# Two transformer layers on one core: the opening written out block by block, nine and ten leading tiles, and large shared tiles

## The chip, the cores and the metric

The kernel runs on one core of a Trainium2 chip. Its time is the device time of one execution in microseconds (us); of several runs the median is given. The core has engines with instruction queues of their own: TensorE (PE in the profile, with PEld for its weight loads), VectorE (DVE), ScalarE (ACT), GpSimd (POOL), and the queue that issues the transfers (SP). Semaphores tie them together. Each engine takes its instructions in order, so an instruction that waits holds up all that stand behind it in its queue.

## The reference

Sixteen meta tokens are put ahead of 512 tokens, which gives L = 528 rows of width 1024. Each of two layers does this to the rows h:

```python
proj = rmsnorm(h, pre_mix_norm) @ w_in           # 1024 x 3600
#  columns: rq rk rv rg (retention, 4 heads of 128), gq gk gv gr (gated linear attention, 4 heads), ga (16 wide)
merged = concat(retention(rope(rq), rope(rk), rv) normed * silu(rg),
                gla(gq, gk, gv, decay from ga) normed * silu(gr))
h = h + rmsnorm(merged @ w_out, post_mix_norm)
u = rmsnorm(h, pre_ffn_norm) @ ffn_up            # 1024 x 5632
a, g = split(conv3(u))                           # causal, width 3, per column
h = h + rmsnorm((gelu(a) * g) @ ffn_down, post_ffn_norm)
```

RMSNorm divides each row by the root of its mean square and multiplies it by a gain for each column. The output is h without the meta tokens.

## The kernel before, in words

Activations lie transposed: 128 columns of the model on the partitions (KD = 8 blocks k of them), tokens along the row. Every wide product is made of three half-precision products, since weights and activations are each split into a high and a low half (`product`, L361 to L363: high*high, high*low, low*high; each over the eight blocks k, so 24 matmuls for a tile of 128 output columns). The tokens go in two parts, 0 to 232 and 232 to 528 (`SPLIT`), because a product of all 528 doesn't fit one bank of the accumulator. A weight block of 1024 x 128 is loaded as 512 KB into a stage buffer (`Block.load`, L89) and made a "unit" by ScalarE (high half, L105) and VectorE (low half, L106). The ten-odd units ahead of the current one are fetched early (`AHEAD`).

At the start of each layer's mixer the first `LEAD` = 7 tiles of the projection are multiplied with the first part of the tokens alone, and only then with the second part; after them each tile takes both parts in turn (`seq` in `mixer`). The tile list begins with the narrow tile ga (`project_rank`, L540: 16 matmuls), then gk, gk, gq, gq, and four gv; the tenth is the first rk, whose eviction applies the rotation tables. While the second part's norm is still being worked out, the leading tiles are TensorE's work. In layer 0 the norm of the input is special: `start` loads the rows, squares them (`squares`), forms 1/rms on GpSimd (`rstd`, L300), scales the rows by it (`ys`, L408 and L409), transposes the scaled rows block by block (`first_part`, L437), and evicts them as high and low halves of xh with the gain. Tokens 256 to 528 go another way (`first_xh`): the raw rows are transposed into h (`raw_h`, L483), the norms are spread over the partitions by a product of ones with a diagonal (`spread`, L462 and L463), and h is multiplied by them (`scaled`, L471, then `split`, L304 and L305). The raw first part is transposed into h as well, later. At the end of each layer `norms` does the same for the residual: sums of squares over columns (`sumsq`, L327 to L332), `token_rstd` (L316, L300, L462, L463), addition to h on GpSimd (L347), and again for the next norm.

Order: a scheduler with a model of the times sets the order of each engine's queue, from the order in which the program writes the work and from its own clock. In `start` alone the written order is kept, for ScalarE, VectorE and SP, not for TensorE. The load of the identity matrix (`constants`, L242) stands ahead of that region, so the scheduler places it.

Memory: a pool `gen` has 41 slots of one size, out of which nearly everything is taken (rows of the input, projections, `m`, `u`, `ca` and `cg` of the convolution, `ffa`, the tables); `keep` holds xh; `small` has short rings for each name.

## Time and profile before

| | |
|---|---|
| median of 3 runs | 1273.3 us (1272.73 to 1276.95) |
| the profiled execution, its own time | 1271.71 us |
| its span | 1269.8 us |
| TensorE busy | 1239.7 us (98%) |
| VectorE, ScalarE, GpSimd busy | 819.8, 642.0, 167.6 us |
| mean granted TensorE clock | 0.992 |

A chain of waits is the work that ended last, followed back from the end. A group of instructions is all that come from one line with one shape; "mean" is the time of one. Matmuls overlap, so a matmul row of 0.26 us may stand every 0.10 us: the step from one start to the next is what a matmul costs. TensorE's clock is granted at full (1.0) or half rate (0.5).

### The profile page before, as it was taken

The page shows a single profiled execution, that of the slowest core. Times are in us where ns is not written, and L with a number is a line of the kernel's source. Part 1 is how long each engine was busy: PE and PEld are TensorE (multiplying, and loading weights), DVE is VectorE, ACT ScalarE, POOL GpSimd, SP SyncE. Part 2 cuts the span into 40 slices and gives each one's busy share as a digit, 9 for nine tenths or more (in the row PEclk, how much of TensorE's full clock was granted, in tenths as well). Part 3 has the DMA queues.
Part 4 walks back from the last instruction along what each step waited for, and adds up shares of the span by engine and source line. Part 5 has one row for each costly group of instructions (what it writes and reads, how often), then busy time and mean ns, then how long its engine had stood idle before and what let it go on. Part 6 is the DMA issues. An engine that isn't in the chain of part 4 may idle for free.

```text
span 1269.8 us, 26401 instructions
## 1 busy us (share of the span) xinstructions
PE 1239.7 (98%) x11090; PEld 1019.8 (80%) x11090; DVE 819.8 (65%) x1510; ACT 642.0 (51%) x1200; POOL 167.6 (13%) x218
## 2 busy tenths in 40 slices
PE   8999999999999999999988999999999999999997
PEld 6777788888788888888876787888898888886443
DVE  5578845457876666512286688454478867887875
ACT  6664444354855555423255644343548656664541
POOL 1013310044000000000141132100430000000000
PEclk8999999999999999999998999999999999999999
DMA  9731222222433342214152322222215333304651
GB/s 258 212 87 55 68 67 67 68 72 63 133 102 98 101 125 79 88 47 120 32 139 67 84 68 68 64 68 71 84 50 146 108 102 103 126 1 165 200 191 67
DMA packets 206971, 124.26 MB, mean 98 GB/s; under 512 B 6704, under 2 KB 194276, under 8 KB 206852
## 3 DMA queue, kind: packets, MB, share of 16 engines
q1 hardware_dynamic: 206692, 122.04, 32.6%
q8 instruction: 87, 1.43, 0.5%
q0 software_dynamic: 160, 0.52, 0.2%
q14 instruction: 32, 0.26, 0.1%
HBM read 120.45 MB, written 2.10 MB: 97 GB/s over the span
## 4 chain that ended last, share of the span: by engine, by line
PE 80%; DVE 8%; ACT 3%; issue 3%; POOL 2%; DMA 1%; SPq 1%; DVEq 0%; POOLq 0%; ACTq 0%
PE pu L362 12%; PE pu L363 12%; PE pu L361 12%; PE pj L361 6%; PE pj L363 6%; PE pj L362 6%; PE pl L1047 5%; PE pd L362 3%; PE pd L361 3%; PE pd L363 3%; PE po L361 2%; PE po L362 2%; PE po L363 2%; DVE unit L106 2%; PE o L590 1%
## 5 line engine op out<-in xcount | busy, mean ns | idle before, releaser
L362 PE MATMUL pu<-xh,unit 128*128 128x296 f16 (+2 forms) x1408 | 385.7, 275 | 2.0 <-DVE xh L305 2.0
L363 PE MATMUL pu<-xh,unit 128*128 128x296 f16 (+2 forms) x1408 | 385.7, 275 | 0.0
L361 PE MATMUL pu<-xh,unit 128*128 128x296 f16 (+2 forms) x1408 | 384.0, 275 | 0.8 <-ACT xh L304 0.8
L106 DVE SCALAR_TENSOR_TENSOR unit<-st,unit 128x1024 f16<-128x1024 f32 (+1 forms) x186 | 227.5, 1226 | 214.5 <-ACT unit L105 207.8
L361 PEld LDWEIGHTS <-unit 128*128 128x128 f16 x2912 | 285.8, 98 | 48.8 <-issue 5.6
L363 PEld LDWEIGHTS <-unit 128*128 128x128 f16 x2912 | 285.6, 98 | 45.5 <-issue 2.9
L362 PEld LDWEIGHTS <-unit 128*128 128x128 f16 x2912 | 286.3, 98 | 44.5 <-issue 2.2
L105 ACT ACTIVATE unit<-st 128x1024 f16<-128x1024 f32 (+1 forms) x186 | 191.7, 1034 | 138.7 <-PE pu L363 48.7
L361 PE MATMUL pj<-xh,unit 128*128 128x296 f16 (+2 forms) x896 | 248.6, 279 | 1.8 <-ACT gaT L541 1.8
L363 PE MATMUL pj<-xh,unit 128*128 128x296 f16 (+2 forms) x896 | 248.8, 278 | 0.0
L362 PE MATMUL pj<-xh,unit 128*128 128x296 f16 (+2 forms) x896 | 248.6, 278 | 0.0
L934 ACT ACTIVATE u<-pu 128x296 f32<-128x296 f32 (+2 forms) x176 | 66.2, 379 | 99.3 <-PE pu L363 99.2
L363 PE MATMUL pd<-ffa,unit 128*128 128x232 f16 (+1 forms) x352 | 96.8, 276 | 0.0
L361 PE MATMUL pd<-ffa,unit 128*128 128x232 f16 (+1 forms) x352 | 96.8, 276 | 0.0
L362 PE MATMUL pd<-ffa,unit 128*128 128x296 f16 (+1 forms) x352 | 96.7, 276 | 0.0
L332 POOL TENSOR_TENSOR acc<-acc,sq 128x296 f32<-128x296 f32 (+2 forms) x36 | 32.4, 900 | 344.8 <-ACT sq L330 344.1
L300 POOL TENSOR_TENSOR rs_r<-rs_t,every 128x1 f32<-128x1 f32 (+5 forms) x33 | 37.2, 1131 | 279.5 <-DVE rs_t L297 99.5
L923 DVE SCALAR_TENSOR_TENSOR ca<-u,every,ca 128x527 f32<-128x527 f32 (+1 forms) x88 | 66.8, 759 | 10.8 <-ACT ca L918 9.6
L363 PE MATMUL po<-merged,unit 128*128 128x296 f16 (+2 forms) x256 | 69.9, 275 | 0.0
L362 PE MATMUL po<-merged,unit 128*128 128x296 f16 (+2 forms) x256 | 69.9, 275 | 0.0
L923 DVE SCALAR_TENSOR_TENSOR cg<-u,every,cg 128x527 f32<-128x527 f32 (+1 forms) x88 | 66.6, 757 | 4.9 <-ACT cg L918 4.3
L361 PE MATMUL po<-merged,unit 128*128 128x296 f16 (+2 forms) x256 | 69.6, 275 | 0.0
(218 smaller groups left out, 1535.6 us busy)
## 6 DMA issues: line engine op xcount, KB each, us to landing
st<-in_ffn_up SPq DMA_DIRECT2D x88, 512.0 KB, 3.8
st<-in_w_in SPq DMA_DIRECT2D x56, 512.0 KB, 4.0
st<-in_ffn_down SPq DMA_DIRECT2D x46, 512.0 KB, 3.9
st<-in_w_out SPq DMA_DIRECT2D x16, 512.0 KB, 3.6
st<-in_ffn_down SPq DMA_DIRECT2D x8, 384.0 KB, 5.5
out<-yo SPq DMA_DIRECT2D x8, 256.0 KB, 2.0
xt<-in_x SPq DMA_DIRECT2D x6, 256.0 KB, 3.6
w<-in_ffn_down SPq DMA_DIRECT2D x3, 512.0 KB
```

Of the source, the lines that this page charges most:

```text
L105: nc.scalar.activation(u[:, 0], st, AF.Copy, scale=SW)
L106: nc.vector.scalar_tensor_tensor(out=u[:, 1], in0=st, scalar=SW, in1=u[:, 0], op0=ALU.mult, op1=ALU.subtract)
L300: nc.gpsimd.tensor_tensor(out=r[:w, :n], in0=t[:w, :n], in1=self.mhalf[:w, :n], op=ALU.pow)
L332: eng.tensor_tensor(out=acc[:, :n], in0=acc[:, :n], in1=sq[:, :n], op=ALU.add)
L361: nc.tensor.matmul(ps[:, :n], w[:, 0, kk, :], x[:, 0, n0:n1], start=i == 0, stop=False)
L362: nc.tensor.matmul(ps[:, :n], w[:, 0, kk, :], x[:, 1, n0:n1], start=False, stop=False)
L363: nc.tensor.matmul(ps[:, :n], w[:, 1, kk, :], x[:, 0, n0:n1], start=False, stop=i == tot - 1)
L590: nc.tensor.matmul(o[:, i, :], intra(i), vn(i), start=i == 0, stop=i == 0, skip_group_check=i > 0)
L923: nc.vector.scalar_tensor_tensor(out=to, in0=u[:, max(lo, d) - d : L - d], scalar=self.cvec[:, ci(i) : ci(i) + 1], in1=to, op0=ALU.mult, o ...
L934: nc.scalar.activation(u[:, n0:n1], ps[:, : n1 - n0], AF.Copy, scale=IXW)
L1047: mm = lambda x, w, **kw: nc.tensor.matmul(ps, x, w, skip_group_check=more, **kw)
```

## The change

It has four parts.

The opening (layer 0). The raw rows of tokens 0 to 256 are transposed at once, ahead of their norms, into four tiles of the accumulator, and copied from there into h. The scaled rows `ys` go. In their place a block k of the normed, transposed rows is a product: the raw rows are the stationary operand, a diagonal matrix of 1/rms the moving one (`wave`, `columns`). Each block is evicted as before, and goes straight into the products of the first two tiles, ga and the first gk. Blocks are written two ahead. After that `opening` does the second part of the tokens in steps, one ahead of each further leading tile: squares, raw transposes, spread, multiplication, and the fetch of one more weight block each.

The order. The region of written order now holds TensorE too, and lasts until the leading tiles of layer 0 have had their first part. Within it a tile fetches nothing ahead (`ahead` = 1); the steps do. The tables, gains and constants are worked on behind it; the rows of gains are loaded earlier.

The lead. Nine tiles lead in layer 0, and ten in layer 1.

The memory. xh, the last layer's rest of weights and its gains share one place `xroom` in the constants' tile; kq, the tables and the mixer's short rings share one tile `room` with `av` (all activations ahead of the down-projection); `m` is one tile; `u` has ten buffers of its own, and `ca` and `cg` three in all. In `ffn_down` the sums of squares are added by VectorE every time, no longer by GpSimd but for the last.

```diff
-LEAD = 7
+LEAD = (9, 10)
 ULEAD = 5
-MIX = (3, 7)
...
+KINDS = (("rs_t", 10, 4), ("rs_r", 10, 4), ("sst", 1, 4))
+MIXKINDS = (("vnt", P, 6), ("mv", 20, 4), ("bst", 6, 8), ("ms", 10, 4), ("ont", P, 8), ("dgrt", 16, 4), ("dgt", 32, 2))
...
-        xh = self.keep.tile([P, KD, 2, L], F16, tag="xh", name="xh", bufs=1)
+        xh = self.xroom.bitcast(F16).rearrange("p (k i n) -> p k i n", k=KD, i=2)
...
+    def load_first(self):
+        nc = self.nc
+        self.xs = []
+        self.load_x(0)
+        self.load_x(1)
+        rows = self.g([P, P], F32, "rows")
+        nc.sync.dma_start(rows[:16, :], self.a["pre_mix_norm"].rearrange("l (t p) -> (l t) p", p=P))
+        for j in range(3):
+            self.blocks[j].load()
+        self.load_x(2)
+        self.blocks[3].load()
+        self.load_x(3)
+        self.load_x(4)
+        for j in range(4, 7):
+            self.blocks[j].load()
+        self.load_gains()
+        return rows
...
+        pts = [self.mx([P, 2, HALF], "ptx") for _ in range(4)]
         for t in range(2):
-            self.squares(t, ys[t])
+            self.squares(t, [self.g([P, 512], F32, "yt") for _ in range(2)])
+            for k in range(KD):
+                nc.tensor.transpose(pts[k // 2][:, k % 2, P * t : P * t + P], self.xs[t][k // 4][:, k % 4 * P : (k % 4 + 1) * P], self.ident)
+        self.raw_first = lambda b: nc.scalar.activation(self.h[:, 2 * b : 2 * b + 2, :HALF], pts[b], AF.Copy)
         r = [self.row_rstd(t) for t in range(2)]
         self.first_gains(rows)
         self.blocks[0].fetch()
-        for t in range(2):
-            nc.scalar.activation(ys[t][0], self.xs[t][0], AF.Copy, scale=r[t][:, 0:1])
-            nc.vector.tensor_scalar(out=ys[t][1], in0=self.xs[t][1], scalar1=r[t][:, 0:1], scalar2=None, op0=ALU.mult)
+        self.raw_first(0)
+        self.raw_first(1)
+        self.dgs = [self.diagonal(r[t][:, 0:1], P) for t in range(2)]
         self.blocks[1].fetch()
+
+    def wave(self, gaT, evac):
+
+        nc = self.nc
+        u0, u1 = self.blocks[0].unit, self.blocks[1].unit
+        p0, p1 = self.mm([P, WN], "pj"), self.mm([P, WN], "pj")
+
+        def columns(k):
+            pt = self.mx([P, WN], "pts")
+            for t in range(2):
+                nc.tensor.matmul(pt[:, P * t : P * t + P], self.xs[t][k // 4][:, k % 4 * P : (k % 4 + 1) * P], self.dgs[t], start=True, stop=True)
+            gain = self.pars[:, R_PRE + k : R_PRE + k + 1]
+            nc.scalar.activation(self.xh[k][:, 0, :HALF], pt[:, :HALF], AF.Copy, scale=gain)
+            nc.vector.scalar_tensor_tensor(out=self.xh[k][:, 1, :HALF], in0=pt[:, :HALF], scalar=gain, in1=self.xh[k][:, 0, :HALF],
+                                           op0=ALU.mult, op1=ALU.subtract)
+
+        for k in range(2):
+            columns(k)
         for k in range(KD):
-            self.first_part(k, ys, 0, 2, 0, HALF)
-            if k in MIX:
-                self.blocks[2 + MIX.index(k)].fetch()
+            if k + 2 < KD:
+                columns(k + 2)
+            self.rank_step(p0, u0, k, 0, SPLIT)
+            self.product_step(p1, u1, k, self.xh[k], 0, SPLIT, k == 0, k == KD - 1)
+            if k in (1, 3):
+                self.raw_first(2 + k // 2)
+            if k == 4:
+                self.blocks[2].fetch()
+        nc.scalar.activation(gaT[:, :SPLIT], p0[:, :SPLIT], AF.Copy, scale=IXW)
+        evac(p1[:, :SPLIT], 0, SPLIT)
+
+    def opening(self):
+
+        nc = self.nc
+        n = L - HALF
+        rs = {}
+
+        def square(t):
+            self.squares(t, [self.g([P, 512], F32, "yt") for _ in range(2)])
+            rs[t] = self.row_rstd(t)
+
+        def raw(*ks):
+            for k in ks:
+                pt = self.mx([P, WN], "pth")
+                for t in range(2, 5):
+                    c0, w = CHUNKS[t]
+                    nc.tensor.transpose(pt[:, c0 - HALF : c0 - HALF + w], self.xs[t][k // 4][:w, k % 4 * P : (k % 4 + 1) * P], self.ident[:w, :w])
+                nc.scalar.activation(self.h[:, k, HALF:], pt[:, :n], AF.Copy)
+
+        def part(b):
+            t = self.sm([P, 2, WN], "tmp2", bufs=2)[:, :, :n]
+            nc.vector.tensor_tensor(out=t, in0=self.h[:, 2 * b : 2 * b + 2, HALF:], in1=bc[:, None, :n].to_broadcast([P, 2, n]), op=ALU.mult)
+            for i in range(2):
+                k = 2 * b + i
+                gain = self.pars[:, R_PRE + k : R_PRE + k + 1]
+                nc.scalar.activation(self.xh[k][:, 0, HALF:], t[:, i], AF.Copy, scale=gain)
+                nc.vector.scalar_tensor_tensor(out=self.xh[k][:, 1, HALF:], in0=t[:, i], scalar=gain, in1=self.xh[k][:, 0, HALF:],
+                                               op0=ALU.mult, op1=ALU.subtract)
+
+        square(2)
+        self.blocks[3].fetch()
+        yield
+        square(3)
+        square(4)
+        self.blocks[4].fetch()
+        yield
+        raw(0, 1)
+        bc = self.mx([P, WN], "nbc")
+        for t in range(2, 5):
+            c0, w = CHUNKS[t]
+            self.spread(bc[:, c0 - HALF : c0 - HALF + w], rs[t][:w, 0:1], w)
+        self.blocks[5].fetch()
+        yield
+        for b in range(4):
+            if b < 3:
+                raw(2 * b + 2, 2 * b + 3)
+            part(b)
+            if 6 + b < LEAD[0]:
+                self.blocks[6 + b].fetch()
+            yield
+        self.blocks[LEAD[0]].fetch()
+        yield
...
+    def diagonal(self, r, w):
+        dg = self.sm([P, P], "ndg")[:w, :w]
+        self.nc.vector.tensor_scalar(out=dg, in0=self.ident[:w, :w], scalar1=r, scalar2=None, op0=ALU.mult)
+        return dg
...
+        room = cell(self.keep, [P, 6 * L + sum(n * c for _, n, c in MIXKINDS)], F32, "av", "room", 1)
+        self.cosT, self.sinT = room[:, 4 * L : 5 * L], room[:, 5 * L : 6 * L]
+        self.ring(room[:, 6 * L :], MIXKINDS)
...
-        kq = [cell(self.gen, [P, 2, L], F32, "kq", "kq", 2) for _ in range(2)]
+        kq = [room[:, 2 * L * pr : 2 * L * (pr + 1)].rearrange("p (i n) -> p i n", i=2) for pr in range(2)]
...
-        self.spawn(self.tables())
+        if l:
+            self.spawn(self.tables())
         self.rate = TICK
-        seq = [(t, 0) for t in TILES[:LEAD]] + [(t, 1) for t in TILES[:LEAD]] + [(t, hf) for t in TILES[LEAD:] for hf in range(2)]
+        lead = LEAD[l]
+        seq = [(t, 0) for t in TILES[:lead]] + [(t, 1) for t in TILES[:lead]] + [(t, hf) for t in TILES[lead:] for hf in range(2)]
         for i, ((nm, h), half) in enumerate(seq):
-            if i == LEAD:
-                self.finish(self.later)
+            if i == lead:
+                if l:
+                    self.finish(self.later)
+                else:
+                    next(self.first_steps)
+                    self.region.__exit__(None, None, None)
+                    for gen in (self.tables(), self.gains(), self.mixer_constants()):
+                        self.spawn(gen)
+            ahead = AHEAD
+            if l == 0 and i < lead:
+                if i == 0:
+                    self.wave(gaT, evac(*seq[1][0]))
+                if i < 2:
+                    continue
+                next(self.first_steps)
+                ahead = 1
+            u = self.block(l, nm, h, ahead=ahead)
             if nm == "ga":
-                self.project_rank(self.block(l, nm, h), gaT, half)
+                self.project_rank(u, gaT, half)
             else:
-                self.project(self.block(l, nm, h), evac(nm, h), half, base if nm in ("rq", "gq", "gr", "rg") else 0)
+                self.project(u, evac(nm, h), half, base if nm in ("rq", "gq", "gr", "rg") else 0)
...
-                us[key, i] = self.g([P, L], F32, "u")
+                us[key, i] = cell(self.gen, [P, L], F32, "u", "u", 2 * ULEAD)
...
-            ca = self.g([P, L], F32, "ca")
-            cg = self.g([P, L], F32, "cg")
+            ca, cg = (cell(self.gen, [P, L], F32, "c", nm, 3) for nm in ("ca", "cg"))
...
-                t = self.g([P, 2, L], F16, "ffa")
-                self.split(t, cg[:, lo:], lo, L)
-                av.append(t)
+                if col == 0:
+                    keep["av"] = self.keep.tile([P, KF, 2, L], F16, tag="av", name="av", bufs=1)
+                self.split(keep["av"][:, col], cg[:, lo:], lo, L)
+                av.append(keep["av"][:, col])
...
-                    self.sumsq(accs[half], ct, m[ct][:, n0:n1], n1 - n0, ct == KD - 1)
+                    nc.scalar.activation(m[:, ct, n0:n1], ps[:, : n1 - n0], AF.Copy, scale=IAW)
+                    self.sumsq(accs[half], ct, m[:, ct, n0:n1], n1 - n0, True)
...
-        with self.tc.manual_schedule(engines={mybir.EngineType.Activation, mybir.EngineType.DVE, mybir.EngineType.SP}):
-            self.start()
-        self.later = self.first_xh(2, 5, HALF, L)
-        for gen in (self.later, self.gains(), self.mixer_constants(), self.raw_h(0, 2, 0, HALF)):
-            self.spawn(gen)
+        self.region = self.tc.manual_schedule(engines={mybir.EngineType.Activation, mybir.EngineType.DVE, mybir.EngineType.SP, mybir.EngineType.PE})
+        self.region.__enter__()
+        self.start()
+        self.first_steps = self.opening()
```

`load_x` takes the chunk as an argument and loads it; `load_gains` is the loading half of what was `gains`; `product_step` and `rank_step` are the bodies of the loops of `product` and `project_rank`. `first_part`, `first_xh` and `raw_h` go.

182 lines of the change are left out of this document (80 added, 102 removed).

## The prediction

> **What bounds the kernel now.** I read the page first, then the stretches of the span, then what TensorE waits for.
>
> ```profile
> span 1269.8 us, 26401 instructions
> PE 1239.7 (98%) x11090; PEld 1019.8 (80%) x11090; DVE 819.8 (65%) x1510; ACT 642.0 (51%) x1200; POOL 167.6 (13%) x218
> PE 80%; DVE 8%; ACT 3%; issue 3%; POOL 2%; DMA 1%; SPq 1%; DVEq 0%; POOLq 0%; ACTq 0%
> ```
>
> TensorE is busy for 98% of the span and holds 80% of the chain of waits. An edit pays only where it takes away idle time of TensorE, time at half clock, or TensorE work. The stretches that matter are these (the columns are span, then busy time and instructions of PE, PEld, DVE, ACT, POOL, then granted clock, DMA share, GB/s):
>
> ```profile
> 0.00:60.00 60.00, 52.85 (x395) 43.90 (x396) 32.57 (x70) 35.45 (x74) 6.91 (x19) 0.91 0.84 237
> 11.90:18.60 6.70, 6.38 (x32) 4.96 (x32) 5.16 (x10) 5.02 (x11) 1.79 (x2) 0.51 0.89 256
> 29.00:32.30 3.30, 3.30 (x20) 2.55 (x19) 1.39 (x3) 3.30 (x12) 0.00 (x0) 0.53 1.00 289
> 672.30:677.40 5.10, 2.30 (x16) 1.70 (x17) 2.11 (x8) 1.11 (x4) 0.86 (x1) 0.98 0.00 0
> 677.50:684.20 6.70, 6.03 (x25) 3.50 (x25) 6.70 (x16) 4.34 (x9) 0.00 (x0) 0.51 0.01 2
> ```
>
> Half clock follows idle time twice in the opening (0.51, 0.53) and once between the layers (0.51). The last two stretches are where layer 0's closing norm meets layer 1's lead. Everywhere else TensorE is nearly full, so I price the opening and that boundary, and ask of the rest only whether it turns into a wait.
>
> **The opening before.** First its useful work, from TensorE's groups up to 60 us and its steps in time:
>
> ```profile
> L361 PE MATMUL pj<-xh,unit 128*128 128x232 f16 (+1 forms) x83 | 23.7, 291 | 1.8 <-ACT gaT L541 1.8
> L363 PE MATMUL pj<-xh,unit 128*128 128x232 f16 (+1 forms) x82 | 23.7, 289 | 0.0
> L362 PE MATMUL pj<-xh,unit 128*128 128x232 f16 (+1 forms) x82 | 23.6, 288 | 0.0
> L540 PE MATMUL pj<-xh,unit 128*128 128x232 f16 (+1 forms) x32 | 7.7, 306 | 0.3 <-ACT xh L439 0.3
> L483 PE MATMUL pth<-every,xt 128*128 128x128 f32 (+1 forms) x40 | 6.7, 269 | 0.0
> ```
>
> ```profile
> 18.47 0.26 PE L362 MATMUL pj<-xh,unit 128*128 128x232 f16 x1
> 18.77 0.26 PE L363 MATMUL pj<-xh,unit 128*128 128x232 f16 x1
> 57.79 0.29 PE L362 MATMUL pj<-xh,unit 128*128 128x296 f16 x1
> 58.29 0.29 PE L363 MATMUL pj<-xh,unit 128*128 128x296 f16 x1
> ```
>
> ```profile
> 44.38 0.66 PE pth L483 x6
> 104.69 1.98 PE o L590 x16
> ```
>
> A matmul of 232 costs 0.10 us at full clock (three steps in 0.30), one of 296 costs 0.125 (four in 0.50), a raw transpose 0.11 (0.66/6). A full-precision product of 128 by 128 shows as two records of 0.124 (1.98/16), so 0.25. By 60 us the kernel has done 279 projection matmuls: the first part of seven tiles (16 + 6 x 24 = 160, 16.0 us), 119 of the second part (14.9 us), 40 raw transposes (4.4), and some 2 us of gains, spread and gate products. That is 37.3 us; 22.7 of the first 60 us are lost to waiting, half clock and work that only the opening needs.
>
> **The opening after.** What starts the first projection?
>
> ```profile
> 9.31 1.06 POOL L300 TENSOR_TENSOR rs_r<-rs_t,every 128x1 f32<-128x1 f32 x2 [8.19 <-DVE sst L428]
> 10.44 0.23 PE L247 MATMUL ptc<-every,rows 16*128 16x16 f32 x1 [2.92 <-DMA every<-in_c_ident]
> 11.23 2.46 POOL L109 COPY unit<-unit 128x256 f16<-128x256 f16 x3 [0.87 <-DVE unit L106]
> 13.74 0.10 PEld L540 LDWEIGHTS <-unit 128*128 128x128 f16 x1 [0.66 <-POOL unit L109]
> ```
>
> Not the scaled rows: TensorE's first projection at 13.74 waits for GpSimd's three copies of the narrow unit, which follow the gains and so the identity's arrival at 10.4. Dropping `ys` gives nothing here. The diagonals follow 1/rms (done at 10.4) and are ready at about 11, and three blocks k are multiplied while the copies run. What matters more is the identity. It now stands ahead of 16 transposes in a written TensorE order. If the scheduler moves its load forward, among the first rows, the transposes run at 8.4 to 10.2 and the narrow unit is copied by 13.4; if it stays where it is, they end near 12.5 and the copies near 15.5. The load's consumer is now at the head of the longest chain, so I take 13.4 and keep 15.5 as the other bound.
>
> Then TensorE does in order: five more blocks (ten products of 0.25, 2.5 us) and 40 projection matmuls (4.0 us), 6.5 us at full clock. Idle time before 13.4 makes me keep half clock to 18.7, as now: 2.65 of it is done by then, and the rest ends at 22.6. The 16 products cost 4.0 us where 16 transposes cost 1.8; the 16 raw transposes of the first part go from behind 44 us, where they cost 1.8, into idle time.
>
> The Trainium skill, TensorE: Matmul & The Clock Gate, section Terms, calls the transpose mode four times faster for single precision, where my rows give 0.25 against 0.11, a factor of 2.3. By its factor a block's two products would cost 0.88 instead of 0.50 and the sum would be 1.9 us worse; no run here has shown the pair on the same data yet.
>
> Seven tiles follow (2.4 us each, 16.8), with 24 raw transposes (2.6) and the spread (0.7): 20.1 us if nothing waits. Something does, because the next unit is made one step ahead, behind the eviction of the last tile:
>
> ```profile
> L105 ACT ACTIVATE unit<-st 128x1024 f16<-128x1024 f32 x9 | 9.5, 1050 | 5.1 <-DMA st<-in_w_in 5.1
> L484 ACT ACTIVATE every<-pth 128x272 f32<-128x272 f32 (+1 forms) x11 | 3.9, 378 | 1.5 <-PE pth L483 1.5
> L304 ACT ACTIVATE xh<-tmp 128x272 f16<-128x272 f32 x8 | 3.4, 430 | 2.3 <-DVE tmp L471 2.2
> L424 ACT ACTIVATE yt<-xt 128x512 f32<-128x512 f32 (+1 forms) x3 | 1.8, 617 | 0.0
> L823 ACT ACTIVATE kq<-pj 128x232 f32<-128x232 f32 x4 | 1.4, 343 | 1.0 <-PE pj L363 1.0
> ```
>
> ```profile
> L106 DVE SCALAR_TENSOR_TENSOR unit<-st,unit 128x1024 f16<-128x1024 f32 x4 | 4.9, 1221 | 2.5 <-ACT unit L105 2.5
> ```
>
> After a tile ends, ScalarE evicts it (0.34), squares rows (0.62 and a short read) or copies two raw blocks (0.76) and makes two high halves (0.86), and only then the unit's high half (1.05), behind which VectorE makes the low half (1.22). Behind the wave that is two evictions, one square and the unit: tile 3's low half is ready about 3.8 us on, with tile 2 done at 2.4, a wait of 1.4. Followed through the steps, tile 6 waits 0.7, tile 8 waits 1.3, the others fit; about 3.0 us in all. The lead ends at 22.6 + 20.1 + 3.0 = 45.7 us. Useful work done by then: 16 + 8 x 24 = 208 matmuls (20.8), 40 raw transposes (4.4) and the spread (0.7), 25.9. Lost: 19.8, against 22.7. **The opening gains 2.9 us.** The 1.8 us behind `gaT`'s eviction (in the first L361 row) are among what goes: ScalarE stood there behind a unit whose weights were late (5.1 us of such idle time in its L105 row); now x and seven blocks are asked for in one row, without another queue's wait between. Bounds: no waits and full clock from 15.3 give another 4.7 us (loss 15.1); the late identity costs 1.1 (half of 2.1, as half clock covers it), and two more stretches of half clock 3.4, so a loss of 1.6 against before.
>
> **The boundary of the layers.**
>
> ```profile
> PE pj L540 <- ACT xh L304: 2.5, 2, 1.7
> PE pj L540 <- DVE xh L305: 1.7, 2, 1.4
> PE nbc L463 <- DVE ndg L462: 1.6, 1, 1.6
> PE nst L316 <- DVE acc L332: 1.3, 1, 1.3
> ```
>
> ```profile
> 678.55 1.22 DVE L305 TENSOR_TENSOR xh<-tmp,xh 128x296 f16<-128x296 f32 x3
> 681.79 1.60 DVE L305 TENSOR_TENSOR xh<-tmp,xh 128x296 f16<-128x296 f32 x4
> ```
>
> The seven tiles' first part is used up at 672.3. Till 677.5 TensorE is busy for 2.3 of 5.1 us, then creeps at half clock until 684.1. Those 11.8 us hold 16 small records (1.9 us) and 25 matmuls of 296 (3.2): 6.7 are lost. Ten leading tiles put 72 more matmuls of 232 there, 7.2 us, up to 681.4. By then most blocks of xh are made (678.5 to 683.4, one in 0.7 us), and three tiles in flight use one in 1.0 us (8 x 0.125), so TensorE never catches up. Ahead of these blocks now stand the evictions of three tiles (0.34 each on ScalarE), one of them with the rotation (two VectorE passes like those on xh, 0.4 each): 1 to 2 us of delay that the 1.0 against 0.7 absorbs. I leave 0.5 for what remains. **The boundary gains 6.2 us**; nothing, if the norm's chain is late by another 7 us; 6.7 at most, and 1.3 more if the sums of squares on VectorE shorten the wait for `acc`. That move I set at nothing, since VectorE, which takes the additions from GpSimd, has a full queue there too; ±1.3.
>
> **The memory.** Shared places cost nothing unless a new owner waits. The mixer's `room` waits for the last reader of `av`, layer 0's last down-projection, while kq is first written when layer 1's second tile is evicted; the tables' load waits likewise, and the tenth tile needs them only near 680. xh's memory was single before. `ca` and `cg` go from many slots to three:
>
> ```profile
> L923 DVE SCALAR_TENSOR_TENSOR ca<-u,every,ca 128x527 f32<-128x527 f32 (+1 forms) x20 | 15.3, 767 | 2.6 <-ACT ca L918 2.2
> L918 ACT ACTIVATE ca<-u,every 128x528 f32<-128x528 f32 x10 | 8.3, 828 | 0.3
> L985 DVE SCALAR_TENSOR_TENSOR cg<-ca,cg 128x528 f32<-128x528 f32 x9 | 6.4, 709 | 1.0
> L305 DVE TENSOR_TENSOR ffa<-cg,ffa 128x528 f16<-128x528 f32 x9 | 6.3, 702 | 0.0
> L974 ACT ACTIVATE ca<-ca 128x528 f32<-128x528 f32 x9 | 5.7, 631 | 0.0
> ```
>
> Wholly in a row a pair of columns takes 2 x (0.83 + 2 x 0.77) + 0.63 + 0.71 + 0.63 + 0.70 = 7.4 us, while TensorE needs 48 x (0.10 + 0.125) = 10.8 for it. Nothing.
>
> **Sum.** 1271.7 (the profiled execution) - 2.9 - 6.2 = 1262.6. The median stood 1.6 above that execution, so **1264 us**.
>
> **Rivals.** (1) The written order costs what it saves: late identity, and idle time in each step that brings half clock back twice. The opening loses 1.6, the boundary stays: 1273.3 + 1.6 - 6.2 = 1269. For it: a wait of 1.8 us was enough for half clock (29.0 to 32.3). Against: 0.7 to 1.4 is shorter. (2) The opening runs freely, with the clock back early: 1273.3 - 7.6 - 6.2 = 1259.5. For it: up to 18.6 TensorE is busy for 6.38 of 6.70 us and still at half clock; what is new before 15.3 are real products. The same page of the Trainium skill (TensorE: Matmul & The Clock Gate, Part 4: PE-mode transpose) says that transposes don't count as activity for the clock; by that rule the products would bring it back one step earlier, and this trace agrees as far as it goes. (3) The boundary gives nothing, because VectorE, with 6.70 of 6.70 us busy there, takes the three tiles' evictions and the additions ahead of xh: 1273.3 - 2.9 = 1270. (4) Slower: the three slots tie `cg` of one pair to the end of the pair before, and the units of that time (two, 2.1 us ScalarE, 2.4 VectorE) and four evictions (1.4) fall into the same row: 7.4 + 2.4 + 1.4 = 11.2, and with each semaphore's lag more. It decides from 10.8 on: each 0.5 us over costs 17 pairs x 2 layers x 0.5 = 17 us, less the gains of 9.1, so 1281. Against: the flush may be placed first, which leaves only half of the row tied.
>
> **Chances and range.** Forecast 0.47, (1) 0.20, (2) 0.15, (3) 0.10, (4) 0.08. Within 0.3% (3.8 us: 1269.5 to 1277) is about what this kernel's runs can't tell from no change. Faster by more: the forecast, (2), half of (1), a third of (3), 0.76; the same 0.16; slower 0.08. Range 1256 to 1271, which leaves out (4) and the edge of (2).
>
> **What would show it.** Right: TensorE's first projection at 13.4, the lead's end at 45 to 46, no wait of TensorE and no half clock between 670 and 690, no new wait in the up-projections. Wrong: the identity's wait before 16 transposes, a granted clock near 0.5 beyond 20 us, TensorE waiting for `cg`'s or `u`'s place, or the tenth tile waiting for its tables.

## The result, and the profile after

The change makes the kernel slower. Its median is 1280.9 us (1279.2 to 1281.6, 7 runs) against 1272.7 us (1270.5 to 1277.0, 7 runs) beside it on the same chip; the ratio is 1.0058, with a 95% interval of 1.0044 to 1.0073. The forecast was 1264 us, faster. From the page of the changed kernel, whose own time was 1280.9 us:

```profile
span 1279.2 us, 26402 instructions
PE 1238.6 (97%) x11106; PEld 1018.2 (80%) x11106; DVE 827.5 (65%) x1518; ACT 640.8 (50%) x1194; POOL 161.5 (13%) x206
...
PE 79%; DVE 9%; ACT 4%; DMA 3%; issue 2%; POOL 2%; SPq 0%; DVEq 0%; POOLq 0%; ACTq 0%
```

TensorE is busy for about as long as before (1238.6 us against 1239.7), so the 9.4 us by which the span is longer are idle time; time at half clock counts as busy. To find where both lie I priced each TensorE record of a trace by its form (the lower quartile of the step from such a record to the next, over both traces; a wait for a semaphore is part of the form). The warm-up, the products with the diagonals and the transposes of the scaled rows count as nothing. The sum of the prices up to a moment is then taken away from that moment. What is left is the time lost so far, in us:

```
up to us                60    240    640    700    740    860    940   1160   1260
before                23.0   46.0   49.0   61.9   69.5   85.1   87.6   87.7   88.5
after                 18.0   43.5   46.7   50.9   60.2   84.6   91.1   91.2   97.2
after minus before    -5.0   -2.5   -2.3  -11.0   -9.3   -0.5   +3.5   +3.5   +8.7
```

Read it by columns. The opening gains 5.0, of which 2.5 are left at the end of the first mixer. The boundary of the layers (640 to 700) gains 8.7. Then the second mixer and the beginning of its output projection (700 to 940) give back 14.5, and the last down-projection (from 1160) 5.2. The up-projections (940 to 1160) change nothing. The table depends a little on the forms: with the shape alone as the form the opening gains 3.9 instead of 5.0, and the later stretches gain or lose what they do here within 0.4.

Opening and boundary, in the stretches of the changed kernel and in what TensorE waits for between 640 and 720 (columns as in the prediction):

```profile
0.00:60.00 60.00, 55.65 (x450) 48.30 (x452) 33.36 (x67) 35.22 (x70) 6.83 (x19) 1.00 0.85 235
670.00:677.00 7.00, 7.00 (x74) 6.91 (x73) 3.00 (x10) 2.17 (x6) 0.85 (x1) 1.00 0.01 2
677.00:684.00 7.00, 7.00 (x57) 5.10 (x55) 6.84 (x16) 4.25 (x10) 1.07 (x1) 1.00 0.00 0
```

```profile
PE pj L621 <- ACT every L324: 1.7, 1, 1.7
PE pj L621 <- DVE every L325: 0.5, 1, 0.5
```

The clock of the first 60 us is 1.00 where it was 0.91, and the half clock between the layers is gone. So both things that were meant to pay did. The waits of TensorE between 700 and 960 show where it went; after, and then before:

```profile
PE lps L818 <- ACT lvx L867: 5.8, 7, 1.6
PE lps L818 <- DVE lvx L868: 2.4, 2, 1.2
PE pto L718 <- DVE on L706: 1.5, 1, 1.5
PE rst L743 <- DVE on L708: 1.1, 1, 1.1
```

```profile
PE pu L362 <- DVE xh L305: 1.0, 2, 0.6
PE ptv L557 <- ACT gv L823: 0.8, 1, 0.8
PE kv L677 <- ACT kn L576: 0.7, 1, 0.7
...
PE lps L738 <- DVE lvx L788: 0.3, 1, 0.3
```

`lps` are the small products of the seven levels of the gated linear attention. Each level's product needs what VectorE and ScalarE made of the level before, so this is a chain with waits in it, which runs beside the projections: a generator, "side work", of which the mixer writes two steps behind each tile part (`TICK` = 2 in `tick`). Before, nearly every wait of this chain was covered by a projection, and `lps` waits 0.6 us in all; after, it waits 8.2. The first mixer, where nine tiles lead in place of seven, shows the same on a smaller scale: from 60 to 260 us `lps` waits 4.0 us, and 0.8 before. The groups of the output projection show the other half of it. After, and then before, in the time from the last projection to the up-projection:

```profile
L675 PE MATMUL o<-sn,rq 128*128 128x128 f32 (+1 forms) x8 | 1.6, 276 | 0.0
L718 PE MATMUL pto<-every,on 128*128 128x128 f32 x4 | 1.3, 328 | 1.5 <-DVE on L706 1.5
```

```profile
L638 PE MATMUL pto<-every,on 128*128 128x128 f32 x1 | 0.3, 273 | 0.0
L638 PE MATMUL pto<-every,ont 16*128 16x16 f32 x1 | 0.2, 230 | 0.0
```

Side work of the last heads (`o`, `pto`) is left over when the projections are used up: 23 TensorE instructions of `o` and `pto` come after the last projection, 5 before the change. They run without cover, and the output projection (`po`) waits 0.7 us that it did not wait before.

In the last down-projection there is one longer wait and half clock behind it. After (waits from 1190 on, and the stretches round them), and then before:

```profile
PE pl L1150 <- ACT part L1160: 2.5, 1, 2.5
PE hp L1189 <- DVE yo L1168: 1.3, 1, 1.3
```

```profile
1191.50:1194.50 3.00, 0.84 (x4) 0.38 (x4) 3.00 (x4) 3.00 (x7) 0.00 (x0) 0.98 0.11 40
1194.50:1198.00 3.50, 3.50 (x10) 1.28 (x9) 2.51 (x3) 1.42 (x3) 0.00 (x0) 0.53 0.00 0
```

```profile
PE pl L1047 <- ACT part L1057: 0.7, 1, 0.7
```

### The profile page after: what moved, and what is told of

Read it like the earlier page. It is cut to its first block, busy times and chain, and to the rows that moved or that the text cites. A ratio compares the mean times of both kernels' runs of the same rounds, so it can differ in the third digit from the quotient of the medians.

```text
span 1279.2 us, 26402 instructions
## 1 busy us (share of the span) xinstructions
PE 1238.6 (97%) x11106; PEld 1018.2 (80%) x11106; DVE 827.5 (65%) x1518; ACT 640.8 (50%) x1194; POOL 161.5 (13%) x206
## 4 chain that ended last, share of the span: by engine, by line
PE 79%; DVE 9%; ACT 4%; DMA 3%; issue 2%; POOL 2%; SPq 0%; DVEq 0%; POOLq 0%; ACTq 0%
PE pu L387 12%; PE pu L388 12%; PE pu L386 12%; PE pj L386 6%; PE pj L388 6%; PE pj L387 6%; PE pl L1150 3%; PE pd L386 3%; PE pd L388 3%; PE pd L387 3%; DMA st<-in_ffn_down 2%; DVE unit L110 2%; PE po L386 1%; PE po L387 1%; PE po L388 1%
## 5 line engine op out<-in xcount | busy, mean ns | idle before, releaser
L387 PE MATMUL pu<-every,unit 128*128 128x296 f16 (+2 forms) x1408 | 385.4, 274 | 2.1 <-DVE every L325 2.1
L388 PE MATMUL pu<-every,unit 128*128 128x296 f16 (+2 forms) x1408 | 385.4, 274 | 0.0
L386 PE MATMUL pu<-every,unit 128*128 128x296 f16 (+2 forms) x1408 | 383.7, 274 | 0.8 <-ACT every L324 0.7
L110 DVE SCALAR_TENSOR_TENSOR unit<-st,unit 128x1024 f16<-128x1024 f32 x184 | 228.2, 1240 | 162.6 <-ACT unit L109 160.1
L109 ACT ACTIVATE unit<-st 128x1024 f16<-128x1024 f32 x184 | 191.4, 1041 | 134.7 <-PE pu L388 52.7
L386 PE MATMUL pj<-every,unit 128*128 128x296 f16 (+2 forms) x896 | 247.3, 276 | 1.4 <-DVE room L831 1.0
L388 PE MATMUL pj<-every,unit 128*128 128x296 f16 (+2 forms) x896 | 246.8, 276 | 0.7 <-DVE unit L110 0.7
L387 PE MATMUL pj<-every,unit 128*128 128x296 f16 (+2 forms) x896 | 247.3, 276 | 0.0
L388 PE MATMUL pd<-av,unit 128*128 128x232 f16 (+1 forms) x352 | 96.9, 276 | 0.0
L387 PE MATMUL pd<-av,unit 128*128 128x296 f16 (+1 forms) x352 | 96.8, 276 | 0.0
L386 PE MATMUL pd<-av,unit 128*128 128x232 f16 (+1 forms) x352 | 96.7, 276 | 0.0
L352 DVE TENSOR_TENSOR acc<-acc,sq 128x296 f32<-128x296 f32 (+2 forms) x60 | 33.3, 556 | 75.1 <-ACT sq L350 73.2
L320 POOL TENSOR_TENSOR every<-every 128x1 f32<-128x1 f32 (+5 forms) x33 | 38.8, 1177 | 298.5 <-DVE every L317 124.4
L1150 PE MATMUL pl<-unit,fk 128*128 128x512 f16 x330 | 73.2, 385 | 2.5 <-ACT part L1160 2.5
```

The source lines that it names most:

```text
L109: nc.scalar.activation(u[:, 0], st, AF.Copy, scale=SW)
L110: nc.vector.scalar_tensor_tensor(out=u[:, 1], in0=st, scalar=SW, in1=u[:, 0], op0=ALU.mult, op1=ALU.subtract)
L320: nc.gpsimd.tensor_tensor(out=r[:w, :n], in0=t[:w, :n], in1=self.mhalf[:w, :n], op=ALU.pow)
L352: eng.tensor_tensor(out=acc[:, :n], in0=acc[:, :n], in1=sq[:, :n], op=ALU.add)
L386: nc.tensor.matmul(ps[:, :n], w[:, 0, kk, :], x[:, 0, n0:n1], start=first, stop=False)
L387: nc.tensor.matmul(ps[:, :n], w[:, 0, kk, :], x[:, 1, n0:n1], start=False, stop=False)
```

## Experiments

Ratios are to the kernel before, run beside each on the same chip.

**Which part gives back? e1 to e4.** Theory S: the further leading tiles take filler from the side chain, which then isn't covered. Rival M: the shared rooms tie buffers together and cause the waits.

```diff
 e1, the changed kernel             e2, the kernel before
-LEAD = (9, 10)                    -LEAD = 7
+LEAD = (9, 7)                     +LEAD = (7, 10)
```

> The changed kernel with seven leading tiles in layer 1 in place of ten; nothing else differs. Theory S (side chain): the ten tiles gain about 9 us at the boundary of the layers, but they use up projections that TensorE needs as filler while VectorE works on the gated attention's levels; so here the boundary's waits and its half clock come back (some 8 us lost again by 700 us), and the 8.7 us that layer 1's mixer gave back and the 3.6 us in its output projection go: 1277 to 1281, much the same time. Theory M (memory): the waits for the levels come from the shared place room, so they stay, and the boundary's loss is added: 1287 to 1290.

> The kernel before with ten leading tiles in layer 1; nothing else differs, its memory and its opening are the old ones. Theory S: the boundary gains 8 us or so by 700 us, and the mixer and the output projection behind it give back 8 to 12: 1270 to 1277. Theory M: nothing is given back, 1264 to 1266.

e1: 1275.2 us, ratio 1.0004 (0.9993 to 1.0015). e2: 1280.8 us, ratio 1.0042 (1.0026 to 1.0058). Ten tiles alone make the old kernel slower, without any shared room, and without them the new one is even with the old. The longest waits of e2 between 700 and 960 are those of the changed kernel within a tenth of a microsecond:

```profile
PE lps L738 <- ACT lvx L787: 5.8, 7, 1.6
PE lps L738 <- DVE lvx L788: 2.4, 2, 1.2
PE pto L638 <- DVE on L626: 1.4, 1, 1.4
PE rst L663 <- DVE on L628: 1.1, 1, 1.1
```

M falls for the mixer. Both times lie outside the numbers that S gave (1277 to 1281 for e1, 1270 to 1277 for e2): S had counted 12.3 us of loss behind the boundary in the changed kernel, where the table has 14.5.

```diff
 e3, the kernel before
-        self.ahead = QAHEAD
+        self.ahead = QAHEAD if what not in ("w11", "t1") or kk < WFIRST else min(QAHEAD, WFIRST + 1)
 e4, the changed kernel
-TICK = 2
+TICK = 3
```

> The kernel before with the one line of the last down-projection's early fetch from the change (seven blocks ahead in place of eight where the weights go into xh's place). If this line makes the changed kernel's tail 5 us longer, 1277 to 1279, with TensorE's wait for the eviction of the partial products at 2.5 us; if the tail comes from the order in which the shared tile lets the conversions run, no change, 1272 to 1274.

> The changed kernel, with three steps of the side work written behind each part of a tile in place of two (in both layers' mixers). Theory S: the side chain is written earlier among the projections, so more of them are left behind it as filler, nothing is left for the output projection, and its 3.6 us and part of the 8.7 go: 1270 to 1277. Theory M: the waits for the levels stay, 1279 to 1283.

e3 takes over a line of the change that the section on it does not show: the early fetch of the last stage reaches seven blocks ahead, not eight. e3: ratio 1.0006 (0.9990 to 1.0021), no change that can be told. In its profiled execution the last stage is 105.2 us long, from the first to the last record of `pl`, against 103.9 before, and `pl` waits 1.9 us for `part`, against 0.7. So this is at most a part of that loss. e4: 1310.6 us, ratio 1.0288 (1.0266 to 1.0310): three steps everywhere are far too many. By 140 us it has lost 47.1 us, where the changed kernel has lost 34.0. This was a miss, far above the 1270 to 1277 expected: "write side work earlier" is not right as such.

**The last stage: e5, e6, e7.** The addresses in the two built programs show a difference that no line of the diff tells. The loads of the last stage go to these places:

```
before  180416 184640 188864 193088 197312 and 126240 (right behind wrest, which takes 116000 to 126240)
after   201312 205536 209760 213984 218208
```

Five places are asked for; the kernel before has a sixth in the rest of the buffer that `wrest` leaves free, because every block is placed wherever there is room. The fixed `xroom` has taken that away. The loads of t1 and t2 then run dry: in the kernel before, the third block of t2 is asked for 5.2 us after the stage's first product, in the changed one 9.2 us. Theory P: this makes the last stage slower. Rival R: the order of loads and conversions does, wherever they lie.

```diff
 e5, the changed kernel (e6: with LEAD = (9, 7) as well), in Quarter.load
+        if st is None and self.what == "t1" and self.kk == HK - 1:
+            c0 = (HK - WFIRST + 2) * 512
+            st = self.kern.xroom[:, c0 : c0 + 512].rearrange("p (k c) -> p k c", c=512)
 e7, the kernel before
-            self.wrest = self.keep.tile([P, HK - WFIRST, 512], F32, tag="xh", name="wrest", bufs=1)
+            self.wrest = self.keep.tile([P, KD * L], F32, tag="xh", name="wrest", bufs=1)[:, : (HK - WFIRST) * 512].rearrange("p (k c) -> p k c", c=512)
```

> The changed kernel with one line of data moved: the load of t1's last row block (128 x 512 numbers) goes to the unused end of the room xroom instead of taking one of the five staging places. Theory P (the last stage is slower because the kernel before had a sixth staging place there, in the rest of the buffer that wrest left free, and the large shared room took it away): the load of the third t2 block is issued some 5 us after the last stage's start and not 9, the wait of TensorE for part falls from 2.5 us to about the 1.9 of the run with only the smaller reach, no half clock follows, and the time falls by 3 to 5 us to 1276-1278. Rival R (the order of the loads and of the conversions, not their places, holds the loads up): no change, 1280-1282.

> The same place given back, with seven tiles leading in the second layer. P: the last stage's loss goes here too (it was 6.9 us, 2.4 in the kernel before with the smaller reach), so 1270-1272, under both kernels. R: 1275 as with seven tiles alone.

> The kernel before, with its buffer wrest made as large as the buffer of xh whose room it takes, so that nothing else can lie in the rest: five staging places in the last stage instead of six; no instruction is added or taken away. P: the last stage loses 3 to 5 us as in the changed kernel, 1276-1278, ratio about 1.003. R: no change, 1272-1274.

e5: 1279.2 us, ratio 1.0048 (1.0033 to 1.0063). e6: 1273.6 us, 1.0001 (0.9990 to 1.0012). e7: 1274.6 us, 1.0011 (1.0001 to 1.0020). The loads did what P says: the third block of t2 is asked for 2.0 us after the stage's first product in e5, and 8.0 us after it in e7. By the ratios the place is worth 1.3 us (e5 against the changed kernel), 0.4 (e6 against e1) and 1.4 (e7 against the kernel before), and later 1.8 (e11 against e13). All have the sign that P gives, and the three that were forecast (3 to 5 us) are about a third of that or less; only e7 is clear of no change by its own interval. In the profiled executions the last stage is 103.9 us long before, 105.5 without the sixth place (e7), 109.1 after, 105.4 with it given back (e5), 108.0 in e6. These lengths hold time at half clock too: one stretch of 3.4 us, which costs 1.7, in the changed kernel and in e6, none in the other three. Nor does the place end the wait for `part`: 2.5 us after, but 2.0, 2.3 and 2.7 in e5, e6 and e11, which have it back. So the place is one part of that loss, and half clock another; the reach of e3 may be a third, and the rest isn't settled.

**How many tiles? e8 and e10.** e8 is e6 with LEAD = (9, 8). e10 is e6 with LEAD = (8, 7), for which the opening's first two steps were put into one.

> As e6 with eight tiles leading in the second layer. Theory S (each further leading tile starts the chain of side steps one tile part later, so what the boundary gains the second mixer gives back, and more): between the kernels with seven and with ten, about a third of the way, 1272-1274. Rival B (the first further tile covers most of the boundary's wait, and the give-back comes with the later ones): at or under the kernel with seven, 1268-1270.

> The kernel of e6 with eight tiles leading in the first layer instead of nine (two steps of squares of the opening are put into one step). Theory S: the first layer's mixer gave back 3.5 us of the opening's 5 because its chain of side steps starts two tile parts later than before; with one fewer it gives back about half, and the opening loses less than 1 us: 1271-1273. Rival O: the opening needs all nine tiles as cover, the steps of the second half's columns come too late for the second pass: 1275-1278.

e8: 1275.4 us, ratio 1.0016 (1.0001 to 1.0030), between seven and ten as S said, though above its 1272 to 1274. e10: 1281.9 us, ratio 1.0080 (1.0061 to 1.0098), the rival's way and beyond its 1275 to 1278: the opening itself now waits, and the clock from 14 to 60 us is 0.93 where it was 1.00. So, as it is written, the opening is slower with eight tiles as cover. But by the table of lost time that is the smaller part: e10 has lost 3.0 us more than e6 by 60 us and 7.7 more by 240 (50.8 against 43.1). What costs the rest in the first mixer wasn't tested.

```profile
PE nbc L548 <- DVE ndg L552: 3.5, 1, 3.5
```

**Only the number of steps? e11, e13, e14, e15, e18.** The chain begins when the fifth tile has its second part, five parts behind the lead, whatever the lead is. Three further leading tiles leave three tile parts fewer after that point, which is six side steps. Theory N: this count is the whole cause. It can be made good without touching the lead:

```diff
 e13, the changed kernel; e11: the same with the place of e5; e18: as e11 with lead + 13;
 e14, the kernel before with LEAD = (7, 10); e15, the kernel before with its LEAD = 7
-            self.tick(TICK)
+            self.tick(TICK + (1 if l and lead + 4 <= i < lead + 10 else 0))
```

> The changed kernel with the place of e5 and ten tiles leading, in which six tile parts of the second layer, from the one where the chain of side steps starts, write three side steps each instead of two (six steps more). Theory N (the chain is late by as many steps as the three further tiles took from it, and only their number counts): the six steps are caught up, nothing is left over for out_proj, 1273-1276. Theory S (the chain is bound by VectorE, so steps written earlier only make TensorE wait at another place): 1279-1285.

> The changed kernel, ten tiles leading, with the six side steps written earlier in the second layer and nothing else. Theory N (the number of steps that the further leading tiles took is the cause): the second mixer and out_proj give back nothing, 1270-1272.5, at or under the kernel before. Theory S (VectorE's own pace is the bound, and e11's gain was the place's and the steps' together): 1275 or more.

> The kernel before with ten tiles leading in the second layer (e2, 1280.8) and the same six steps. N: the boundary's gain of 5 to 6 us stays and the 15 us given back go: 1267-1270, faster than the kernel before. If the shared rooms take part in the cause: it stays above 1275.

> The kernel before with its seven leading tiles and the six steps written earlier in the second layer. N (there was nothing to catch up): no gain, 1272 to 1278, slower if the steps now come before VectorE is ready for them. Rival G (steps written earlier are a gain of their own, whatever leads): 1266-1270.

> The kernel of e11 with nine extra steps instead of six. Theory N (three further tiles take three parts of two steps each, so six is the number): the last three steps come before VectorE is ready for them, as in e15, and cost: 1272-1276. Rival: the chain is still late after six, and nine gain again: 1266-1268.

```
                                     median us   ratio to before (95%)
after, ten lead                        1280.9    1.0058 (1.0044 to 1.0073)
e13  after + six steps                 1273.1    0.9993 (0.9978 to 1.0008)
e5   after + place                     1279.2    1.0048 (1.0033 to 1.0063)
e11  after + place + six steps         1269.7    0.9979 (0.9969 to 0.9989)
e18  after + place + nine steps        1277.8    1.0026 (1.0017 to 1.0035)
e2   before, ten lead                  1280.8    1.0042 (1.0026 to 1.0058)
e14  before, ten lead + six steps      1270.7    0.9981 (0.9970 to 0.9993)
e15  before, seven lead + six steps    1284.5    1.0090 (1.0074 to 1.0106)
```

Six steps are worth 0.6 to 0.7% where ten tiles lead, in three pairs (e13, e11, e14). Where seven lead, the same six cost 0.9%, and with ten, nine cost half a per cent more than six. So it isn't that steps written earlier are good; their number has to fit what leads. The signs are those of N, the sizes are not: none of the five times lies in the range that N gave. Gains were smaller than forecast in e13 and e14 and larger in e11, and the losses of e15 and e18 larger. TensorE's waits from 700 to 960 in e11, and then in e15:

```profile
PE ptv L640 <- ACT gv L908: 2.0, 1, 2.0
PE lps L821 <- ACT lvx L870: 1.2, 2, 0.9
PE pj L389 <- ACT tmp L734: 1.1, 1, 1.1
...
PE lps L821 <- DVE lvx L871: 0.8, 2, 0.5
```

```profile
PE lps L738 <- DVE dgt L751: 2.9, 3, 1.9
PE lps L738 <- ACT lvx L787: 2.0, 2, 1.3
PE ptl L768 <- ACT gv L823: 1.9, 1, 1.9
PE lps L738 <- DVE lvx L788: 1.4, 2, 0.9
```

In e11 `lps` waits 2.0 us instead of 8.2, and 5 instructions of `o` and `pto` are left behind the last projection instead of 23. In e15 `lps` waits 6.3 us: TensorE takes its queue in order, so a product of the chain that is written before VectorE has its operand holds up the projections behind it. The stretches of the second set of levels, after, before, and in e11:

```profile
768.00:793.00 25.00, 19.35 (x298) 13.88 (x296) 21.89 (x52) 9.11 (x17) 10.09 (x14) 0.93 0.15 44
```

```profile
761.00:781.00 20.00, 18.82 (x306) 14.52 (x305) 19.38 (x46) 11.26 (x26) 6.88 (x9) 1.00 0.19 54
```

```profile
754.00:775.00 21.00, 19.76 (x322) 15.85 (x321) 18.64 (x42) 11.86 (x26) 6.28 (x8) 1.00 0.18 51
```

VectorE is at work for most of each (21.89 of 25, 19.38 of 20, 18.64 of 21); what differs is the filler beside it (TensorE 19.35 of 25, with a stretch at half clock in it, against 19.76 of 21). Six steps earlier, this set begins near 755 instead of 769.

S and N are both true in part. By the table of lost time from e11's and e13's traces (columns as above), the second mixer still loses more than before between 700 and 860, by 4.5 and 7.9 us:

```
up to us                60    240    640    700    740    860    940   1160   1260
e11                   18.0   43.4   46.7   50.9   62.0   78.6   81.4   81.4   85.1
e13                   18.0   43.5   46.8   50.9   63.0   82.0   84.9   84.9   88.9
```

Half clock explains the difference of the two: between 700 and 860 us there are 3.4 us of it in e11 and 10.2 in e13, which cost 1.7 and some 5, and none before. Some 3 us are left in both, among them 0.8 us by which `ptv` waits longer than before (2.0 in all against 1.2). Three steps more don't take that rest away, as e18 shows. What it is stays open.

**The smaller terms: e9, e12, e16, e17.**

```diff
 e9: e6, and e17: e11, with the conversions of t2 no more than four blocks ahead
+        if what == "t2":
+            self.ahead = 4
 e12: e6, in ffn_down
-                    self.sumsq(accs[half], ct, m[:, ct, n0:n1], n1 - n0, True)
+                    self.sumsq(accs[half], ct, m[:, ct, n0:n1], n1 - n0, ct == KD - 1)
 e16: e17 with four steps more in the first mixer, for its two further tiles
-            self.tick(TICK + (1 if l and lead + 4 <= i < lead + 10 else 0))
+            self.tick(TICK + (1 if lead + 4 <= i < lead + (10 if l else 8) else 0))
```

> The kernel of e6 (seven tiles lead in the second layer, the sixth place given back) in which the blocks of the product t2 are converted at most four blocks ahead instead of eight. Theory Q: ScalarE's copies of the first products (part), for which TensorE waits 2 us and then falls to half clock, stand behind the conversions of later blocks, written ahead of them; with fewer of those in front the wait goes and with it the half clock: 3 to 4 us faster than e6, 1269-1271. Rival D: ScalarE has to wait for the same loads and sums of VectorE anyway: 1273-1275 as e6.

> The kernel of e6 with the sums of squares of ffn_down as in the kernel before (all but the last multiplication on GpSimd). Measures the one term that the prediction took as nothing, 0 with bounds of 1.3 us to either side: 1272.3-1274.9 if it holds.

> The kernel of e11 with four further steps in the first layer's mixer for its two further leading tiles, and the blocks of t2 at most four ahead. N: the first mixer's give-back of 3.5 us goes too, 1265-1268. If the first mixer is bound otherwise (by VectorE's conversions of the opening): 1269-1271, or slower by new waits.

> The kernel of e11 (six steps, the sixth place) with the blocks of t2 converted at most four ahead. If the wait for part in the last stage goes with it: 1267-1269; if ScalarE waits there for loads and sums anyway, as e9 had it within its uncertainty: 1269-1271.

e9: 1272.5 us, ratio 1.0000 (0.9990 to 1.0010), and e17: 1270.3 us, ratio 0.9971 (0.9960 to 0.9983): neither can be told from e6 and e11, so the reach of t2 isn't shown to matter. In e17's profiled execution the wait for `part` is 0.8 us and not 2.7, but `hp` waits 1.6 us for `yo`, which it did not in e11: the wait moved. e12: 1276.3 us, ratio 1.0028 (1.0016 to 1.0040): putting the sums back on GpSimd costs about 0.27% (3.4 us, above the 1.3 that it was given as a bound; from two ratios with some 0.0012 to either side each, so with some 2 us of doubt). Among it is a wait that e6 doesn't have:

```profile
PE nst L339 <- DVE acc L355: 1.2, 1, 1.2
```

e16: 1270.2 us, ratio 0.9978 (0.9966 to 0.9989), no better than e11. By 140 us it has lost 37.6 where e11 lost 34.0, by 240 they have lost 43.6 and 43.4: in the first mixer steps given earlier only move the loss.

The versions that beat both kernels are e11, e14, e16 and e17, by 0.2 to 0.3% under the kernel before.

## Why the prediction was wrong

**The opening gained more than forecast, 5.0 us by the table against 2.9.** At the prediction's own prices it is 3.9: by 60 us the changed kernel has done 208 and 112 projection matmuls of the two widths, the kernel before 160 and 119, which is 34.8 us of work against 30.9, and as many raw transposes. The first rows of the changed kernel (TensorE, then GpSimd):

```profile
8.19 1.91 PE L437 MATMUL ptx<-every,xt 128*128 128x128 f32 x16
...
11.00 1.73 PE L456 MATMUL pts<-ndg,xt 128*128 128x128 f32 x12 [0.74 <-DVE ndg L550]
12.56 0.26 PE L621 MATMUL pj<-every,unit 128*128 128x232 f16 x1
13.42 0.26 PE L621 MATMUL pj<-every,unit 128*128 128x232 f16 x1 [0.59 <-DVE every L459]
...
20.45 0.26 PE L621 MATMUL pj<-every,unit 128*128 128x232 f16 x1 [1.03 <-DVE every L459]
```

```profile
10.82 1.08 POOL L113 COPY unit<-unit 128x256 f16<-128x256 f16 x3 [0.59 <-DVE unit L110]
```

The identity did move forward, and the transposes ran from 8.2 to 10.1 as supposed. The first projection came at 12.56, not 13.4, since the copies of the narrow unit took 1.08 us and not 2.46; but it stands alone, and the second waited for VectorE until 13.42. The term that was mis-sized is the clock: to "keep half clock to 18.7" was wrong, the clock never fell, so the 2.65 us of that term were not lost. Before, TensorE was busy for 0.91 us of the 3.41 ahead of the fall (8.21 to 11.62); after, at no time under 2.1 in such a stretch of the opening. The wave (the first two tiles, block by block) was done at 20.85 instead of 22.6, though from 13.42 on it waited 1.0 us for VectorE, which the forecast had not. Behind it the waits are 1.0 us and not 3.0, the 1.4 of tile 3 being 0.7 and those of tiles 6 and 8 nothing:

```profile
PE pj L621 <- DVE every L459: 1.6, 2, 1.0
...
PE pts L456 <- DVE ndg L550: 0.7, 1, 0.7
PE pj L388 <- DVE unit L110: 0.7, 1, 0.7
```

The second part's first product is at 43.4 and the last product of the lead at 48.8, interleaved with some 3.4 us of the second part, so the lead took till 45.4 against 45.7. That it comes out is luck. Some 3.4 us stand in the lead that the forecast had not put there: the transposes of the gains and four gate products, and raw transposes at 0.17 us each (1.0 for six) instead of 0.11. They cancel what the clock and the shorter waits saved.

Two products of a block cost 0.46 us, from one row of four records at 13.81 to the next row at 14.27; a transpose 0.12 (1.91/16). That is a factor of 2.0. The factor of four in the Trainium skill, TensorE: Matmul & The Clock Gate, Terms, isn't borne out here: by it, read as against a product, a block is estimated at 0.96.

**The boundary gained more, too: 8.7 against 6.2.** No half clock was left, as forecast. Of waits 2.2 us remained, not 0.5, but the term with the sums of squares, which I set at nothing with 1.3 us as its better end, belonged at that end or beyond it. e12 put the move at 3.4 us, with 2 of doubt and with seven tiles leading; the wait for `acc` that it brings back is 1.2. With ten tiles leading and the sums still on GpSimd, the same table gives the boundary a gain of 7.3 us in e2 and 7.2 in e14, so some 1.4 of the 8.7 come from the move.

**The step that failed** is in the first part: "Everywhere else TensorE is nearly full, so I price the opening and that boundary, and ask of the rest only whether it turns into a wait". I asked this of the memory and of the up-projections. I didn't ask it of the side work, which the sum thus sets at nothing, though the change takes filler from it: 72 matmuls moved to the boundary are 72 matmuls less beside a chain of levels, and six steps less to finish it in. What the runs show in its place is 14.5 us lost between 700 and 940 where the boundary brought 8.7, with `lps` waiting 8.2 us instead of 0.6. Ten tiles alone do this to the kernel before (e2), and six steps written earlier take it back in e13 and e14, but for some 3 us that stay open and for what half clock adds. A full TensorE is no reason to leave a stretch out, where what fills it is itself the cover of a chain.

**"Shared places cost nothing unless a new owner waits"** was wrong in a second way: a place can also vanish that nobody asked for. By the ratios it is 0.4 to 1.8 us of the last stage's 5.2. Half clock, which the forecast had nowhere behind the boundary, is 1.7 of them. The shorter reach of the early fetch stands in no term either.

**The rivals.** (1) fell: the written order cost nothing. (2) was nearest in its mechanism, the clock back early, though the clock never left; but waits remained, and the opening's gain was 3.9 to 5.0, not 7.6. (3) fell. (4), the only slower one, named the three slots of `ca` and `cg`; there is no new wait in the up-projections, whose lost time doesn't move (91.1 to 91.2 from 940 to 1160). It had the right sign for a wrong reason.

**Right by its marks, wrong by its end.** Of the things that "would show it", the lead's end (by luck), the boundary without wait or half clock between 670 and 690 and the quiet up-projections all came. Marks that lie only where a change is meant to pay can't show where it costs.

## What to carry to other kernels

Work moved forward to cover one wait is taken from whatever it covered before: find that second place, and price it as a chain, before counting the gain. Where side work is written at a fixed pace beside the main work, a change of the lead changes how many steps are left for it; try moving the pace with it by the same count (two per tile part here). Of the counts tried, none, six and nine, six was best with ten tiles leading, and none was better than six with seven. And where buffers are placed wherever there is room, a fixed shared room can take away a place that no line of the program names: compare the places that the loads really get.

## What the hardware showed that I had not expected

Half clock does not follow from a wait's length alone. After the wait of 2.5 us for `part` the changed kernel ran at half clock for 3.41 us. In e11 the same product waited longer, and the clock stayed full:

```profile
1184.56 1.67 PE L1153 MATMUL pl<-unit,fk 128*128 128x512 f16 x7 [2.66 <-ACT part L1163]
```

The Trainium skill, TensorE: Matmul & The Clock Gate, Part 1 (What's actually happening), describes a free-running window of about 3.4 us in which activity is counted. The traces agree: in all twenty of this case, every change of the granted clock lies on a grid of 3.41 us, whose first mark differs from one execution to the next (4.80 us before, 6.53 after, 5.66 in e11). Cut along the grid, the changed kernel's wait lies in one window, and that of e11 is shared by two (TensorE is busy for 0.94 us of the first, and for 2.05 and 2.11 of the others):

```profile
1190.96:1194.37 3.41, 0.94 (x6) 0.35 (x4) 3.41 (x4) 3.41 (x6) 0.00 (x0) 1.00 0.23 85
```

```profile
1179.85:1183.26 3.41, 2.05 (x10) 0.83 (x9) 3.41 (x4) 3.41 (x5) 0.00 (x0) 1.00 0.50 154
1183.26:1186.67 3.41, 2.11 (x10) 0.97 (x10) 3.41 (x4) 2.71 (x5) 0.00 (x0) 1.00 0.00 0
```

Over the twenty traces, all 37 windows at full clock with TensorE busy for under 1.5 us were followed by half clock, and none of the 7068 with over 2.6; in between, 33 of 219 were. So whether a wait of this size costs 1.7 us more depends on where the grid happens to lie in that execution, and two profiled executions can differ by that without any cause in the kernel. The advice in the Trainium skill, TensorE: Matmul & The Clock Gate, Why this matters for your kernels, no idle gap above some 3 us, is not strict enough by this trace, where 2.5 us were enough once and 2.7 were not.

The three copies of the narrow unit on GpSimd took 2.46 us before and 1.08 after. Here they are one by one (shortest, median and longest in ns, first and last start in us) with VectorE's pass at that time, in the kernel before and in e2, whose opening is the same:

```profile
L109 POOL COPY unit<-unit x3: 584/587/1387, 11.2 to 12.3; 128x256 f16<-128x256 f16 x3
12.20 1.23 DVE L106 SCALAR_TENSOR_TENSOR unit<-st,unit 128x1024 f16<-128x1024 f32 x1
```

```profile
L109 POOL COPY unit<-unit x3: 395/583/587, 11.4 to 12.4; 128x256 f16<-128x256 f16 x3
12.54 1.38 DVE L106 SCALAR_TENSOR_TENSOR unit<-st,unit 128x1024 f16<-128x1024 f32 x1 [0.30 <-ACT unit L105]
```

The third copy took 1.39 us where it began 0.10 us behind VectorE's pass, and 0.40 in e2, where it began 0.10 us ahead of it. It is the same in the other runs with this opening: 1.39 to 1.46 us behind the pass (e3, e7, e14), 0.40 ahead of it (e15). In the changed kernel all three take 0.39, and the third begins 0.04 us ahead of the pass. So 1.0 of the 1.38 us is a matter of which engine began first; the other 0.4 are the first two copies, 0.58 each beside the row scaling that is gone. The Trainium skill, SBUF — State Buffer, Who interferes with whom, says that such passes on VectorE can hold a port that GpSimd needs for as long as they last. The third copy fits: it ended 0.26 us behind the pass, and TensorE's weight load that waits for it came at 13.74 before and at 12.89 in e2.
